# Softmax heads: 640 key columns per query tile in PSUM banks of 384 and 256 columns instead of 512 and 128

## The chip, the cores and the metric

The kernel runs on one core of one Trainium2 chip. The metric is the device time of one execution in microseconds; the lower the better. The times given are medians of runs on the same chip.

## The reference, cut to what matters

One encoder layer over 2048 positions of width 1024: an adaLN-modulated RMS norm, one input projection, two groups of eight attention heads of width 64, an output projection, and an MLP of width 4096. The first group is stick-breaking attention ("SB" in the kernel), the second is chunked softmax attention ("CA"). The change is in the second group:

```python
qc = q.reshape(B, nc, CHUNK, H, d)                      # CHUNK = 64
s = jnp.einsum('bnqhd,bnkhd->bnhqk', qc, k_band) * (d ** -0.5)   # own chunk + 8 before: 576 keys
s = s + bias[None, None]                                # learned, by clipped relative position
s = jnp.where(valid[None, :, None, None, :], s, NEG_INF)
p = jax.nn.softmax(s, axis=-1)
out = jnp.einsum('bnhqk,bnkhd->bnqhd', p, v_band)
```

Two chunks of 64 queries make a query tile of 128 rows. Their bands, one chunk apart, cover 640 keys together, and the bias table holds a large negative number where a row doesn't see a key. So a query tile of one head needs scores of 128 queries by 640 keys, a row minimum of the negated scores, an exponential, a row sum and a division.

## The kernel before, in words

The kernel is written with a tile framework that assigns buffers, semaphores and the order of most engines' instructions; TensorE instructions are kept in the order in which the program writes them (`pe = Ordered(tc, nc.tensor)`). SyncE's DMA issues in the attention part (`sp = nc.sync`) are not, so the scheduler may place them differently when anything around them changes.

The positions are held in reversed order in four blocks of 512 (`g` = 0 to 3). The attention part is a list of units. A unit is one head and one block `g` of queries (for SB also one block of keys), and it has four steps `qi`, one query tile of 128 rows each. Units come in this order: SB of blocks 2 and 3, CA of blocks 2 and 3, SB of block 1, CA of block 1, SB of block 0, CA of block 0. The CA units of blocks 0, 1 and 2 see 640 keys in each step: 8 heads times 3 blocks make 24 such units and 96 such steps. Those of block 3 have at most 512 keys per step, all in one bank; there are 8 of these units.

The main loop runs one step of a "front" unit, whose scores and softmax are computed, and one of a "back" unit, eight steps behind, whose probabilities are transposed on TensorE (`transposes`), split into two fp32r halves on ScalarE and VectorE (`parts`: tiles `wth`, `wtl`), and multiplied with the values (`values`, tile `acc`). One turn of the loop writes to TensorE, in this order: the transposes of the back unit (up to two tiles `wt` of four 128-column transposes), up to two pairs of value products, the scores of the next front step (`scores`), and a few matmuls of a dense "filler" job (the projections of later blocks, tiles `pf` and `po`), whose number is planned ahead and not decided at run time.

All score and transpose tiles (`z`, `cz`, `ct`, `wt`) come from one PSUM pool of four banks with the tag "z". A bank holds 512 fp32 columns. A new tile takes a bank that the program has released, and its first matmul waits until the last reader of that bank is done.

The scores of a 640-key step lie in two places. `scores(qi)` writes the first 512 keys into a tile `cz` of its own (two matmuls of 512 columns: the queries' high and low halves against the keys). The last 128 keys, the "tail", lie in a tile `ct`, and all four tails of a unit share one bank: `scores(0)` writes them with eight matmuls of 128 columns ahead of `cz`. VectorE reads them with a fused instruction that subtracts the scores from the bias and keeps the row minimum: `tail(qi)` for the tail (tile `s`, from `ct`), and in `soft1(qi)` one for `cz`, which takes the tail's minimum as its start. `soft1(0)` does `tail(0)`, `cz(0)`, `tail(1)`; `soft1(1)` does `cz(1)`, `tail(2)`, and so on; so the `ct` bank is held from `scores(0)` until `tail(3)`, which stands in `soft1(2)`. ScalarE then does the exponential over all 640 columns (tile `e`), GpSimd the division.

All of these instructions carry line L42 in the profile, the line of the helper that records the ordering; they are told apart by their tiles.

Of the kernel before, what the change touches and what calls it, by code (L numbers as in the profile page):

```python
# [9 lines left out]
F32 = mybir.dt.float32  # L10
# [8 lines left out]
P = 128  # L19
# [6 lines left out]
TB = 512  # L26
# [53 lines left out]
def encoder_kernel(ctx, tc, xT, c, g1, g2, w_in, w_rest, gqk, bias, w_o, w1, w2, w_ada, b_ada, out):  # L80
# [2 lines left out]
    pe = Ordered(tc, nc.tensor)  # L83
    osp = Ordered(tc, nc.sync)

    WIN = 640
    cpool = ctx.enter_context(tc.tile_pool(name="cpool", bufs=1))
    dram = ctx.enter_context(tc.tile_pool(name="dram", bufs=1, space=DRAM))
    rp = ctx.enter_context(tc.tile_pool(name="rp", bufs=2))
# [5 lines left out]
    pz = ctx.enter_context(tc.tile_pool(name="pz", bufs=4, space=PSUM))  # L95
# [5 lines left out]
    def scratch(name, shape, *counts):  # L101
        return {i: dram.tile(shape, F32, name=name + "_".join(map(str, i))) for i in product(*map(range, counts))}
# [8 lines left out]
    scr_wo = scratch("scr_wo", [P, 2, KT, P], KT)  # L111
    scr_b = scratch("scr_b", [P, WIN], NH)
    scr_h = dram.tile([P, KT, 2, TB], F32, name="scr_h")
# [19 lines left out]
    def column(tag):  # L133
        small[tag].append(small[tag].pop(0))
        return small[tag][-1]
# [103 lines left out]
    if True:  # L239
# [183 lines left out]
        def prepare_bias(h):  # L423
            b = stp.tile([P, WIN], F32, tag="bg", name=f"b{h}", bufs=2)
            sp.dma_start(b, bias[h])

            def rest():
                pool.memset(b[0:HD, WIN - HD :], NEG)
                pool.memset(b[HD:P, 0:HD], NEG)
                sp.dma_start(scr_b[h,], b)  # L430

            behind.add(4, rest)
# [245 lines left out]
    if True:  # L678
# [16 lines left out]
        def load_k(ca, h, tb, n, nm):  # L695
            k = (kp1 if ca else kp0).tile([P, n * TB], F32R, tag=f"k{ca}", name=f"k{ca}_{h}_{nm}")
            r = (h % 2) * HD
            for i in range(n):
                for l in range(2):
                    ldq.dma_start(  # L700
                        k[l * HD : (l + 1) * HD, i * TB : (i + 1) * TB].bitcast(F32),
                        scr_k[ca, tb + i, h // 2][l, r : r + HD],
                    )
            return k
# [42 lines left out]
        class Unit:  # L747


            def __init__(self, h, g, first, last):  # L750
                self.h, self.g, self.first, self.last = h, g, first, last
                self.nm = f"{self.ca}_{h}_{g}"
                self.ws = []
                self.wt = {}
# [30 lines left out]
        class SB(Unit):  # L785
# [27 lines left out]
            def scores(self, qi):  # L813
                nm = f"{self.nm}_{qi}"
                c0 = qi * P if self.diag else 0
                n = TB - c0
                self.z = z = pz.tile([P, TB], F32, tag="z", name=f"z{nm}")
                qs = slice(qi * P, (qi + 1) * P)
                pe.matmul(z[:, :n], self.q[:, 0, qs], self.k[:, c0:], start=True, stop=False)
                pe.matmul(z[:, :n], self.q[:, 1, qs], self.k[:, c0:], start=False, stop=True)  # L820
# [28 lines left out]
        class CA(Unit):  # L849
            ca = 1  # L850

            def __init__(self, h, g):
                super().__init__(h, g, True, True)
                self.weight = 0.9 * (1 if g < NTB - 1 else 0.75)
                self.nk = min(2 * TB, S - g * TB)
                order = [3] + [kb for kb in (4, 2, 1, 0, 5, 6, 7) if kb < self.nk // P]
                self.blocks = [(kb, max(0, kb - 4), min(4, kb + 1)) for kb in order]

            def load(self):
# [6 lines left out]
                self.k = load_k(1, h, g, nk // TB, f"{g}")  # L866
                self.bt = op.tile([P, WIN], F32, tag="bias", name=f"bias{h}_{g}", bufs=2)
                n = min(WIN, nk)
                sp.dma_start(self.bt[:, :n], scr_b[h,][:, :n])
# [7 lines left out]

            def size(self, qi):
                n = min(WIN, self.nk - qi * P)
                return n, min(n, TB)  # L880

            def scores(self, qi):
                nm = f"{self.nm}_{qi}"
                n, hn = self.size(qi)
                if qi == 0 and n > hn:
                    self.tails = pz.tile([P, TB], F32, tag="z", name=f"ct{nm}")
                    for i in range(STEPS):
                        t = self.tails[:, i * P : (i + 1) * P]
                        ks = slice(i * P + TB, i * P + WIN)
                        for l in range(2):  # L890
                            pe.matmul(t, self.q[:, l, i * P : (i + 1) * P], self.k[:, ks], start=l == 0, stop=l == 1)
                self.z = z = pz.tile([P, TB], F32, tag="z", name=f"cz{nm}")
                ks = slice(qi * P, qi * P + hn)
                for l in range(2):
                    pe.matmul(z[:, :hn], self.q[:, l, qi * P : (qi + 1) * P], self.k[:, ks], start=l == 0, stop=l == 1)

            def tail(self, qi):
                nm = f"{self.nm}_{qi}"
                n, hn = self.size(qi)
                s = zp.tile([P, WIN], F32, tag="p", name=f"s{nm}")  # L900
                m = 3e38
                if n > hn:
                    m = column("m0")
                    t = self.tails[:, qi * P : (qi + 1) * P]
                    dve.tensor_tensor_reduce(s[:, hn:n], t, self.bt[:, hn:n], -1.0, 3e38, ALU.add, ALU.min, m)
                self.sm[qi] = (s, m)

# [240 lines left out]
        STEPS = 4  # L1148
# [145 lines left out]
    if True:  # L1294
# [349 lines left out]
        def plain(mb, i):  # L1644

            f = len(steps)
            steps.extend(Second(mb, i, j) for j in range(NP))
            spread = lambda *ns: [f + n for n in ns]
            if i == 6:
                update(mb, 0, 1, spread(0, 1, 2, 8), spread(4, 5, 6, 12))  # L1650
            if i == 5:
                update(mb, 1, 1, spread(1, 2, 3, 9), spread(6, 7, 8, 13))
                wide = []

                def slot(nm):
                    if not wide:
                        t = raw_pair([P, HK, TB], F32, nm)
                        wide.extend(t[:, n, :] for n in range(HK))
                    return wide.pop(0)

                if mb:
                    update(mb, 0, 0, spread(11, 11, 11, 11), spread(16, 16, 17, 17), slot)
                    update(mb, 1, 0, spread(13, 13, 14, 14), spread(18, 18, 19, 19), kept)
                else:
                    update(mb, 0, 0, spread(11, 12, 13, 14), spread(16, 17, 18, 19))
                    update(mb, 1, 0, spread(15, 16, 17, 21), spread(20, 21, 22, 25), None, True)
            return f
# [115 lines left out]
        def outer(i, plan):  # L1783

            f = len(steps)
            steps.extend(Outer(i, q, k) for q in range(7) for k in range(HP))
            for g in range(HP // 2):
                for pr, (begin, gap) in plan["load"].items():
                    at(begin + gap * g, lambda pr=pr, g=g: half(i, pr, g))
                for pr, (begin, gap) in plan["sum"].items():  # L1790
                    at(begin + gap * g, lambda pr=pr, g=g: half_sum(i, pr, g))
            for q in range(7):
                at(f + HP * q - 12, steps[f + HP * q].load)
            for pr, b in ((5, "22"), (6, "12"), (2, "11"), (4, "21")):
                s = steps[f + HP * OUTER.index(pr)]
                at(f + HP * OUTER.index(pr) + 1, lambda s=s, b=b: s.load_x(b))
            return f
# [47 lines left out]
        for mb in (1, 0):  # L1845
# [3 lines left out]
            for j in range(NP):  # L1849
                f = steps[begin + 7 * j]  # L1850
# [33 lines left out]
        f = plain(0, 1)  # L1884
# [4 lines left out]
        for i, p in ((7, 6), (2, 5), (3, None), (4, None)):  # L1889
            f = outer(i, plan)  # L1890
# [109 lines left out]
```

## Time and profile before

| | before |
|---|---|
| median of 3 runs | 2568.27 us (2566.47 to 2568.61) |
| the profiled execution's own time | 2568.92 us |
| its span, first to last instruction | 2567.2 us |
| TensorE busy | 2534.1 us, 99% |
| VectorE busy | 2012.0 us, 78% |
| ScalarE busy | 1496.2 us, 58% |
| GpSimd busy | 760.8 us, 30% |
| `ct` matmuls, 128 columns | 192 |
| `cz` matmuls, 512 columns | 208 |

Busy time of an engine is the union of its instructions' spans. A TensorE matmul's span is longer than the distance to the next one's start, since they overlap; the cost of a matmul in a stream is the distance between starts, which can be had from a run of n matmuls as (union minus one span) / (n - 1). Of the 208 `cz` matmuls of 512 columns, 192 belong to the 24 units with tails, 16 to block 3.

### The profile page before, as it was taken

The numbers are of one execution on the slowest core, as the hardware profiler recorded it, in microseconds if no ns is written. First come the engines' busy times: TensorE is split into PE (matmuls) and PEld (weight loads), VectorE is DVE, ScalarE is ACT, GpSimd is POOL, SyncE is SP. The second block draws the span as 40 slices with busy tenths as digits, with TensorE's granted clock in tenths as the row PEclk, the third lists the DMA queues.
The fourth block names the chain that finished last, engine by engine and source line by source line (L and its number), as shares of the span: only waits on it lengthen the run. The fifth ranks groups of instructions, "written<-read, shape, count | busy, mean of one in ns | idle before, by whom it ended". The sixth has DMA issues, their size and how long they took to land.

```text
span 2567.2 us, 39419 instructions
## 1 busy us (share of the span) xinstructions
PE 2534.1 (99%) x12436; PEld 2109.1 (82%) x12436; DVE 2012.0 (78%) x3501; ACT 1496.2 (58%) x2871; POOL 760.8 (30%) x1136
## 2 busy tenths in 40 slices
PE   9999999999999999999999999999999999999999
PEld 7888888888888888887887888888888878788887
DVE  7656767887789878998867777668978657988897
ACT  6333435668866687666755555566555545646565
POOL 4330145776776667777612000000000000000000
PEclk9999999999999999999999999999999999999999
DMA  9879978689877788756786888787899779677872
GB/s 351 332 298 363 342 281 293 213 237 290 277 239 233 238 279 272 248 193 196 224 309 243 286 285 274 260 306 267 275 323 304 273 254 409 246 272 265 291 268 82
DMA packets 293200, 698.92 MB, mean 272 GB/s; under 512 B 31360, under 2 KB 83584, under 8 KB 281856
## 3 DMA queue, kind: packets, MB, share of 16 engines
q1 hardware_dynamic: 291696, 691.69, 78.1%
q10 hardware_dynamic: 1296, 4.72, 0.5%
q8 instruction: 98, 1.61, 0.2%
q14 instruction: 110, 0.90, 0.1%
HBM read 477.66 MB, written 218.63 MB: 271 GB/s over the span
## 4 chain that ended last, share of the span: by engine, by line
PE 86%; DVE 5%; ACT 3%; DMA 2%; issue 2%; POOL 1%; SPq 1%; DVEq 0%; POOLq 0%; ACTq 0%
PE ps L42 29%; PE ps_s L42 14%; PE pt L42 11%; PE acc L42 6%; PE wt L42 6%; PE po L42 4%; PE z L42 4%; PE pf L42 4%; PE pq L42 3%; PE cz L42 2%; DVE p L42 2%; PE pso L42 1%; DVE opr L42 1%; PE ct L42 1%; ACT z L42 1%
## 5 line engine op out<-in xcount | busy, mean ns | idle before, releaser
L42 PE MATMUL ps<-h,opw 128*128 128x512 f32 x1512 | 361.7, 392 | 3.6 <-ACT cp L42 3.6
L42 ACT CAST wth<-wt 128x512 fp32r<-128x512 f32 (+3 forms) x544 | 257.4, 484 | 172.4 <-PE wt L42 162.5
L42 POOL TENSOR_TENSOR b<-p 128x512 f32<-128x512 f32 (+1 forms) x320 | 292.5, 914 | 167.9 <-DVE p L42 91.9
L42 PEld LDWEIGHTS ps<-h,opw 128*128 128x128 f32 x1512 | 285.7, 189 | 63.6 <-ACT cp L42 4.0
L42 DVE TENSOR_TENSOR wtl<-wt,wth 128x512 fp32r<-128x512 f32 (+3 forms) x544 | 291.2, 547 | 59.2 <-ACT wth L42 56.7
L42 PE MATMUL pt<-w,ht 128*128 128x512 f32 x1248 | 288.2, 391 | 0.0
L42 PE MATMUL ps_s<-h,opw 128*128 128x512 f32 x1152 | 278.6, 391 | 3.2 <-ACT ps_s L42 3.2
L42 PEld LDWEIGHTS pt<-w,ht 128*128 128x128 f32 x1248 | 233.0, 188 | 47.7
L42 PE MATMUL ps<-oph,opv 128*128 128x512 f32 x1152 | 263.8, 391 | 2.5 <-DVE txo L42 2.5
L42 DVE TENSOR_TENSOR_SCAN p<-z,p,zero 128x512 f32<-128x512 f32 x192 | 245.7, 1281 | 25.6 <-ACT z L42 18.6
L42 PEld LDWEIGHTS ps_s<-h,opw 128*128 128x128 f32 x1152 | 217.1, 189 | 48.8 <-ACT ps_s L42 3.6
L42 PEld LDWEIGHTS ps<-oph,opv 128*128 128x128 f32 x1152 | 217.2, 189 | 48.4 <-DVE txo L42 3.0
L42 PE MATMUL acc<-wth,v 128*128 128x512 f32 (+3 forms) x544 | 220.5, 409 | 0.0
L42 ACT CAST opr<-r 128x512 fp32r<-128x512 f32 x224 | 139.3, 623 | 107.7 <-PE ps L42 51.1
L42 ACT ACTIVATE z<-z 128x512 f32<-128x512 f32 (+1 forms) x320 | 166.5, 521 | 55.2 <-PE z L42 49.3
L42 PE MATMUL z<-k,q 128*128 128x512 f32 (+3 forms) x640 | 185.6, 372 | 7.7 <-DVE p L42 7.2
L42 PE MATMUL acc<-wtl,v 128*128 128x512 f32 (+3 forms) x544 | 185.4, 347 | 0.0
L42 PE MATMUL ps<-opr,ol 128*128 128x512 f32 x768 | 176.4, 389 | 0.1
L42 DVE TENSOR_TENSOR opr<-r,opr 128x512 fp32r<-128x512 f32 x224 | 151.2, 688 | 27.5 <-ACT opr L42 24.8
L42 PE MATMUL wt<-ident,b 128*128 128x128 f32 x1088 | 171.4, 273 | 1.1 <-DVE cols L42 0.3
L42 PEld LDWEIGHTS wt<-ident,b 128*128 128x128 f32 x1088 | 136.3, 140 | 42.2 <-DVE cols L42 1.8
L42 PEld LDWEIGHTS ps<-opr,ol 128*128 128x128 f32 x768 | 144.0, 188 | 30.5 <-DVE ol L42 0.4
(218 smaller groups left out, 4862.8 us busy)
## 6 DMA issues: line engine op xcount, KB each, us to landing
q<-scr_q SPq DMA_DIRECT2D x128, 256.0 KB, 4.7
w<-in_w_dram SPq DMA_DIRECT2D x64, 512.0 KB, 5.8
r<-scr_hid SPq DMA_DIRECT2D x64, 512.0 KB, 7.5
k<-scr_k SPq DMA_DIRECT2D x240, 128.0 KB, 4.3
v<-scr_v SPq DMA_DIRECT2D x120, 256.0 KB, 3.9
wa<-in_w_ada_dram SPq DMA_DIRECT2D x48, 512.0 KB, 6.4
ow<-scr_wo SPq DMA_DIRECT2D x24, 1024.0 KB, 5.8
hw<-scr_hid SPq DMA_DIRECT2D x48, 512.0 KB, 6.4
```

The source lines that it names most:

```text
L42: return lambda *x, **y: self.tc.keep_in_program_order(f(*x, **y))
```

## The change

A step of more than 512 keys is cut at 384 columns (`NEAR`) instead of at 512. The `cz` tile gets the first 384 keys, and the tail is the other 256. Two tails fill a bank, so a unit has two `ct` tiles: `scores(0)` writes the tails of steps 0 and 1, and `scores(1)` those of steps 2 and 3, in each case ahead of that step's own `cz`. The number of matmuls per unit stays at eight for the tails and eight for `cz`, and so does the number of columns that they stream (8 x 640). The VectorE instructions stay the same in number and order, with 256 and 384 columns in place of 128 and 512. A step of at most 512 keys is left as it was: one bank.

```diff
-    WIN = 640
+    WIN, NEAR = 640, 384
...
+                self.tails = {}
...
                 n = min(WIN, self.nk - qi * P)
-                return n, min(n, TB)
+                return n, NEAR if n > TB else n

             def scores(self, qi):
                 nm = f"{self.nm}_{qi}"
                 n, hn = self.size(qi)
-                if qi == 0 and n > hn:
-                    self.tails = pz.tile([P, TB], F32, tag="z", name=f"ct{nm}")
-                    for i in range(STEPS):
-                        t = self.tails[:, i * P : (i + 1) * P]
-                        ks = slice(i * P + TB, i * P + WIN)
+                if qi < 2 and n > hn:
+                    ct = pz.tile([P, 2, WIN - NEAR], F32, tag="z", name=f"ct{nm}")
+                    for i in (2 * qi, 2 * qi + 1):
+                        self.tails[i] = t = ct[:, i % 2, :]
+                        ks = slice(i * P + NEAR, i * P + WIN)
                         for l in range(2):
                             pe.matmul(t, self.q[:, l, i * P : (i + 1) * P], self.k[:, ks], start=l == 0, stop=l == 1)
                 self.z = z = pz.tile([P, TB], F32, tag="z", name=f"cz{nm}")
...
                 if n > hn:
                     m = column("m0")
-                    t = self.tails[:, qi * P : (qi + 1) * P]
+                    t = self.tails.pop(qi)
                     dve.tensor_tensor_reduce(s[:, hn:n], t, self.bt[:, hn:n], -1.0, 3e38, ALU.add, ALU.min, m)
```

The built program's order on TensorE differs in nothing but the second `ct` group of each of the 24 units; VectorE, ScalarE and GpSimd keep their order. On SyncE the scheduler places some loads and stores of the attention part a few positions earlier or later.

## The prediction

> **What bounds the kernel now.** I read the page's busy times and slices first, then the three stretches in which the changed units run, then the groups by shape inside them, then TensorE's waits, and last the timeline of single units.
>
> ```profile
> PE 2534.1 (99%) x12436; PEld 2109.1 (82%) x12436; DVE 2012.0 (78%) x3501; ACT 1496.2 (58%) x2871; POOL 760.8 (30%) x1136
> ...
> PE   9999999999999999999999999999999999999999
> ...
> PE 86%; DVE 5%; ACT 3%; DMA 2%; issue 2%; POOL 1%; SPq 1%; DVEq 0%; POOLq 0%; ACTq 0%
> ```
>
> TensorE is busy in every slice and carries 86% of the chain that ended last. A shorter stream on TensorE is then worth its own length, wherever nothing else runs late in the same stretch. The softmax units with tails lie in three stretches (eight units in each; those of block 3, which stay as they are, lie among the first eight):
>
> ```profile
> core 0: us, PE busy (x) PEld busy (x) DVE busy (x) ACT busy (x) POOL busy (x), PEclk, DMA share, GB/s
> 571.00:701.00 130.00, 126.76 (x773) 108.55 (x772) 95.73 (x357) 107.43 (x268) 92.76 (x92) 1.00 0.92 287
> 883.00:961.00 78.00, 77.39 (x470) 66.19 (x470) 60.61 (x219) 61.00 (x139) 50.76 (x41) 1.00 0.90 279
> 1208.00:1291.00 83.00, 82.89 (x516) 72.19 (x515) 64.83 (x226) 62.53 (x144) 54.75 (x48) 1.00 0.67 204
> ```
>
> The granted clock is 1.00 throughout. TensorE idles 3.24 us in the first, 0.61 in the second and 0.11 in the third. The next engine, ScalarE in the first two and VectorE in the third, is at 83%, 78% and 78%. So the second and third stretch are TensorE's alone; in the first something else is sometimes late. What it is, the waits of that stretch and one place in its timeline say:
>
> ```profile
> PE cz L42 <- DVE cols L42: 1.7, 3, 1.0
> PE wt L42 <- DVE cols L42: 1.4, 2, 1.1
> ...
> 597.68 0.59 ACT L42 CAST stf<-pf 128x512 fp32r<-128x512 f32 x1
> 598.30 0.69 DVE L42 TENSOR_TENSOR stf<-pf,stf 128x512 fp32r<-128x512 f32 x1 [2.58 <-ACT stf L42]
> 598.91 0.74 DVE L42 CUSTOM_DVE_ANT_0 s<-cz,bias,cols 128x512 f32<-128x512 f32 x1
> 599.80 0.41 PE L42 MATMUL wt<-ident,e 128*128 128x128 f32 x2 [1.05 <-DVE cols L42]
> ```
>
> Five waits, 3.1 us, all for a bank that VectorE's score instruction had not yet read. In the one shown VectorE had stood 2.58 us behind ScalarE's eviction of a filler tile, and everything behind it in VectorE's order came late.
>
> **The matmuls.** These are the groups that the change touches, with the two shapes that take their place; block 3 runs those already, with the same operands:
>
> ```profile
> L42 PE MATMUL cz<-k,q 128*128 128x512 f32 x208 | 67.2, 404 | 0.4 <-DVE cols L42 0.4
> L42 PE MATMUL ct<-k,q 128*128 128x128 f32 x192 | 24.8, 272 | 0.7 <-DVE p L42 0.7
> L42 PE MATMUL cz<-k,q 128*128 128x384 f32 x16 | 4.1, 338 | 0.0
> L42 PE MATMUL cz<-k,q 128*128 128x256 f32 x16 | 3.3, 288 | 0.4 <-DVE cols L42 0.4
> ...
> L42 PEld LDWEIGHTS ct<-k,q 128*128 128x128 f32 x192 | 24.2, 191 | 2.5 <-DVE p L42 1.2 <-DVE cols L42 0.3
> ```
>
> The second figure before the bar is one matmul's span, which overlaps the next one's; the distance between starts is the cost. `cz` comes in pairs, `ct` in runs of eight:
> - 512 columns: 67.2 / 104 = 0.646 us for a pair, less 0.404 = 0.242 us.
> - 384 columns: 4.1 / 8 = 0.5125, less 0.338 = 0.1745 us.
> - 256 columns: 3.3 / 8 = 0.4125, less 0.288 = 0.1245 us.
> - 128 columns: 24.8 / 24 = 1.033 for eight, less 0.272, over 7 = 0.109 us.
>
> From 512 to 256 columns the distance falls almost with the columns; from 256 to 128 it falls only from 0.1245 to 0.109. The weight loads of `ct` say why: 24.2 / 24 = 1.008 for eight, less 0.191, over 7 = 0.117 us from load to load. Each of these matmuls has weights of its own, and a 128-column one is over before the next weights are in.
>
> Per unit, eight `cz` matmuls gain 8 x (0.242 - 0.1745) = 0.54 us and eight `ct` matmuls lose 8 x (0.1245 - 0.109) = 0.12 us: 0.41 us gained. Times 24 units: 9.9 us.
>
> The Trainium skill speaks against this: "TensorE: Matmul & The Clock Gate", section "Back-to-back issue gap", gives the isolated distance as N/2.4 + 2.5 ns, in proportion to the columns N, and both kernels stream 5120 columns per unit; by that rule alone the gain would be nothing. The trace does not agree at the short end: 0.109 us at 128 columns, where the rule would have 0.056. The same page's section "LDWEIGHTS (loading the stationary operand)" gives P/1.2 ns, 107 ns for 128 columns of weights, and with that floor the trace agrees.
>
> **VectorE.** The same number of instructions in the same order, with other widths:
>
> ```profile
> L42 DVE CUSTOM_DVE_ANT_0 s<-cz,bias,cols 128x512 f32<-128x512 f32 x96 | 71.7, 747 | 4.5 <-PE cz L42 2.4 <-PE wt L42 0.2
> L42 DVE CUSTOM_DVE_ANT_0 s<-ct,bias 128x128 f32<-128x128 f32 x96 | 27.5, 286 | 4.0 <-PE ct L42 3.2 <-POOL p L42 0.7
> L42 DVE CUSTOM_DVE_ANT_0 s<-cz,bias 128x512 f32<-128x512 f32 x8 | 5.5, 681 | 0.0
> L42 DVE CUSTOM_DVE_ANT_0 s<-cz,bias 128x384 f32<-128x384 f32 x8 | 4.4, 548 | 0.0
> L42 DVE CUSTOM_DVE_ANT_0 s<-cz,bias 128x256 f32<-128x256 f32 x8 | 3.3, 415 | 0.0
> ```
>
> A start value from a column costs 747 - 681 = 66 ns. Before: 286 + 747 = 1033 ns per step. After: 415 for the tail and 548 + 66 = 614 for `cz`: 1029. Nothing in the sum. Inside a unit 130 ns move: the tail of the next step, which stands behind `cz` in a step, gets longer, and `cz`, whose end frees its bank and lets the exponential start, gets shorter. ScalarE's and GpSimd's instructions are untouched.
>
> **The banks.** Before, `cz` of step 1 waits until VectorE has read `cz` of step 0. After, the second `ct` takes that bank, and `cz` of step 1 takes the first `ct`'s, which is free only after `tail(1)`, the next instruction on VectorE. That is the one added wait, 24 times. Behind it on TensorE, in order, stand that step's fillers and the next step's transposes; VectorE and ScalarE wait for these. A usual unit, the first of a stretch and one that waits already show the cover:
>
> ```profile
> 587.59 1.00 PE L42 MATMUL ct<-k,q 128*128 128x128 f32 x8
> 588.63 0.29 DVE L42 CUSTOM_DVE_ANT_0 s<-ct,bias 128x128 f32<-128x128 f32 x1 [0.67 <-PE ct L42]
> 589.15 0.75 DVE L42 CUSTOM_DVE_ANT_0 s<-cz,bias,cols 128x512 f32<-128x512 f32 x1 [0.22 <-PE cz L42]
> 589.82 0.29 DVE L42 CUSTOM_DVE_ANT_0 s<-ct,bias 128x128 f32<-128x128 f32 x1
> 590.87 0.62 PE L42 MATMUL cz<-k,q 128*128 128x512 f32 x2
> ...
> 883.89 0.75 DVE L42 CUSTOM_DVE_ANT_0 s<-cz,bias,cols 128x512 f32<-128x512 f32 x1 [0.24 <-PE wt L42]
> 884.37 0.63 PE L42 MATMUL cz<-k,q 128*128 128x512 f32 x2
> ...
> 903.25 0.75 DVE L42 CUSTOM_DVE_ANT_0 s<-cz,bias,cols 128x512 f32<-128x512 f32 x1
> 903.92 0.29 DVE L42 CUSTOM_DVE_ANT_0 s<-ct,bias 128x128 f32<-128x128 f32 x1
> 904.06 0.73 PE L42 MATMUL cz<-k,q 128*128 128x512 f32 x2 [0.23 <-DVE cols L42]
> ```
>
> In the unit at 588, `scores(0)` shrinks from 8 x 0.109 + 2 x 0.242 = 1.36 us to 4 x 0.1245 + 2 x 0.1745 = 0.85, so TensorE reaches the second `ct` at 590.87 - 0.51 = 590.36, and `cz` of step 1 one `ct` group later, at 590.86. VectorE, which waited 0.67 us for all eight tails, gets the first four matmuls 0.37 us earlier; even with no gain there `tail(1)` ends by 590.11 + 0.13 = 590.24. The wait is covered by 0.6 us. In the unit at 904 TensorE already waits for VectorE. There the second `ct` starts at about 904.0, takes 0.50 us, and `tail(1)`, now 415 ns long, ends at 904.34 inside that time: the added wait costs nothing, but the time saved ahead of it only lengthens the old one, and that unit gains nothing.
>
> That is the loss I set against the gross gain: six waits of this kind (the five and this one). If each eats a unit's 0.41 us, 2.5 us; if VectorE moves with TensorE, none. I take half, 1.2. In the first unit of each stretch, where `cz` of step 1 had a bank that was long free, it now waits for `cz` of step 0: at 884, VectorE is done with that at 884.64, and TensorE gets there at 884.37 - 0.51 + 0.50 = 884.36. That is 0.28 us each if VectorE is no earlier, nothing if it is (less than nothing is excluded, since no wait goes there); I take 0.4 for the three.
>
> **DMA.** SyncE's loads and stores in the attention part move by a few positions. A store that waits for its data holds up the loads behind it, but TensorE loses next to nothing to loads now:
>
> ```profile
> PE po L42 <- DMA ow<-scr_wo: 1.0, 1, 1.0
> ```
>
> It is TensorE's one wait for a load in the attention part. I take nothing, with 1 us to either side for the range.
>
> **Sum.** 9.9 - 1.2 - 0.4 = 8.3 us. From the profiled execution's 2568.9 that gives 2560.6; that execution lies 0.65 us above the median of the three runs, 2568.27, so the forecast for the median is 2560.0 us.
>
> **The rivals.**
> - Swallowed. The first stretch, with ScalarE at 83%, gives nothing back: its waits re-anchor TensorE on VectorE about every 20 us, and each unit's saving turns into a longer wait; the second stretch gives half. For it speaks that the waits are there; against it, that long runs of the first stretch have none and that VectorE and ScalarE wait for TensorE as well (0.67 and 0.22 in the rows above), so they come earlier with it. Gain 3.3 + 1.7 = 5.0, less the 0.4: 4.6, and 2563.7; with the second stretch gone too, 2565.4.
> - The columns decide. If 128 columns cost what their share of 512 does (0.242 / 4 = 0.06 us), eight `ct` and eight `cz` matmuls cost the same before and after: 2568.3. The rows of `ct` matmuls and weight loads, 0.109 and 0.117, speak against it.
> - Slower: the added wait decides. If VectorE, late as at 598, brings `tail(1)` in each unit more than 0.41 us after TensorE could have started `cz` of step 1, the gain is gone; at the 1.05 us of the wait shown, 24 x (1.05 - 0.41) = 15 us, 2584. Against it speak 0.6 us of cover in the usual unit, the unchanged sum on VectorE, and that the second `ct` group runs just ahead of the wait.
>
> **How the numbers follow.** What a measurement of this kernel can tell from no change is about 0.2%, 5.1 us; the bounds are 2563.1 and 2573.4. Forecast with its own scatter 0.78; swallowed 0.12; columns 0.04; slower 0.06. The range takes in the full 9.9 us with 1 us for the loads, 2557.4, and the swallowed case with the second stretch gone, 2565.4. Faster by over 0.2%: 0.79 (the forecast and a little of the swallowed); same 0.15; slower 0.06.
>
> **What would show it.** Right: `cz` of 384 columns with 0.175 us and `ct` of 256 with 0.125 us from start to start, TensorE's busy time 8 to 10 us lower, each of the three stretches shorter by 2 to 3.3 us, VectorE's sum unchanged. Wrong: TensorE's waits for `cols` grown in the first stretch by what the matmuls save (swallowed); `ct` of 256 columns at over 0.17 us (columns); a wait of `cz` for `cols` in nearly every unit (slower).

## The result and the profile after

| | before | after |
|---|---|---|
| median, 19 runs each | 2568.32 us (2565.39 to 2573.41) | 2561.97 us (2558.99 to 2566.52) |
| ratio | | 0.9974, 95% interval 0.9968 to 0.9981 |
| span of the profiled execution | 2567.2 us | 2560.3 us |

The change is 6.4 us faster by the medians, 0.26% by the ratio. The forecast was 8.3 us. A second measurement, on another chip (below), gave 3.3 us: both intervals exclude no change, but the size of the gain, a quarter of a per cent or less, is not far above what single runs scatter by.

The page after, busy time by engine (before, TensorE 2534.1 and VectorE 2012.0):

```profile
PE 2526.9 (99%) x12436; PEld 2109.4 (82%) x12436; DVE 2009.3 (78%) x3501; ACT 1496.6 (58%) x2871; POOL 760.3 (30%) x1136
```

The same count of instructions, 7.2 us less of TensorE. The groups by shape that take the place of the 512 and 128 columns (union of spans, mean span of one, idle time before them), TensorE and then VectorE:

```profile
L42 PE MATMUL cz<-k,q 128*128 128x384 f32 x208 | 54.7, 344 | 0.4 <-DVE cols L42 0.3
L42 PE MATMUL ct<-k,q 128*128 128x256 f32 x192 | 32.0, 290 | 1.7 <-DVE cols L42 1.0 <-DVE p L42 0.7
...
L42 DVE CUSTOM_DVE_ANT_0 s<-cz,bias,cols 128x384 f32<-128x384 f32 x96 | 58.6, 610 | 4.0 <-PE wt L42 0.5 <-PE cz L42 0.2
L42 DVE CUSTOM_DVE_ANT_0 s<-ct,bias 128x256 f32<-128x256 f32 x96 | 40.2, 418 | 1.8 <-PE ct L42 1.5 <-issue 0.3
```

`cz` costs 54.7 / 104 - 0.344 = 0.182 us from start to start (0.1745 forecast). `ct` runs in fours now: 32.0 / 48 = 0.667, less 0.290, over 3 = 0.126 (0.1245 forecast). VectorE has 610 + 418 = 1028 ns per step (1029 forecast).

Where the time went is best read between the same two TensorE instructions of both kernels, which stand in the same order. In the third stretch, from the first unit's first tail product to the last unit's, before and after:

```profile
1205.36 1.11 PE L42 MATMUL ct<-k,q 128*128 128x128 f32 x8 [0.73 <-DVE p L42]
1274.99 1.06 PE L42 MATMUL ct<-k,q 128*128 128x128 f32 x8
```

```profile
1201.31 0.74 PE L42 MATMUL ct<-k,q 128*128 128x256 f32 x4 [0.73 <-DVE p L42]
1268.88 0.69 PE L42 MATMUL ct<-k,q 128*128 128x256 f32 x4
```

69.63 us became 67.57: 2.1 us for seven units. The table does this for each whole stretch, from the TensorE instruction at 568, 880 and 1204 us of the trace of before to the one at 701, 961 and 1292 us, and for the same two instructions in each kernel run below; every distance between two starts is put down to the group of the earlier instruction.

| us | stretch 1 | stretch 2 | stretch 3 | sum | against before |
|---|---|---|---|---|---|
| before | 132.86 | 80.79 | 87.80 | 301.45 | |
| the change | 131.24 | 79.15 | 85.82 | 296.21 | -5.24 |
| the change, second profile | 131.23 | 79.17 | 85.81 | 296.21 | -5.24 |
| 448 and 192 columns | 132.06 | 79.81 | 86.86 | 298.73 | -2.72 |
| 512 and 128, banks of the change | 133.77 | 80.71 | 88.57 | 303.05 | +1.60 |
| own columns first in step 1 | 129.57 | 78.79 | 85.93 | 294.29 | -7.16 |
| the same, second profile | 130.74 | 78.81 | 85.89 | 295.44 | -6.01 |
| half of the tail products left out | 128.50 | 76.96 | 83.91 | 289.37 | -12.08 |
| tails as products of 128 | 136.05 | 83.68 | 91.25 | 310.98 | +9.53 |
| own columns first, copy on VectorE | 136.76 | 81.22 | 89.60 | 307.58 | +6.13 |
| before, VectorE relieved | 130.38 | 80.13 | 87.72 | 298.23 | -3.22 |
| the change, VectorE relieved | 127.85 | 76.81 | 85.59 | 290.25 | -11.20 |

In the change `cz` lost 3.5, 4.1 and 3.6 us in the three stretches and `ct` gained 1.3, 1.4 and 1.1: 7.3 us less in the two groups, of which 5.2 came out at the ends of the stretches (72%). The two profiles of the change agree in each stretch within 0.02 us. The rest of the difference between the two spans lies where nothing was changed: 0.9 us at the start, before the first changed unit, and 0.8 us after the attention part. That part moves from run to run; in the second profile of the change it went 1.8 us the other way.

### The profile page after: what moved, and what is told of

It is laid out like the page before. It is cut to its first block, busy times and chain, and to the rows that moved or that the text cites. A ratio compares the mean times of both kernels' runs of the same rounds, so it can differ in the third digit from the quotient of the medians.

```text
span 2560.3 us, 39412 instructions
## 1 busy us (share of the span) xinstructions
PE 2526.9 (99%) x12436; PEld 2109.4 (82%) x12436; DVE 2009.3 (78%) x3501; ACT 1496.6 (58%) x2871; POOL 760.3 (30%) x1136
## 4 chain that ended last, share of the span: by engine, by line
PE 81%; DVE 8%; DMA 4%; ACT 3%; issue 3%; POOL 1%; SPq 1%; DVEq 0%; ACTq 0%; POOLq 0%
PE ps L42 25%; PE ps_s L42 12%; PE pt L42 11%; PE acc L42 6%; PE wt L42 6%; PE pf L42 4%; PE po L42 4%; PE z L42 4%; PE pq L42 3%; DMA scr_hid<-to 2%; DVE p L42 2%; PE pso L42 1%; PE cz L42 1%; PE ct L42 1%; DMA w<-in_w_dram 1%
```

## The experiments

My theory: a product's cost can't fall below what the load of its weights takes, and under about 256 columns it is set by that load and no longer by its columns; call this the floor. The change takes the tails off the floor, and waits for VectorE swallow part of the gain. The rivals: the widths don't matter, and the gain (or a loss) comes from where banks and loads came to lie; or the added wait is the price that counts.

**Another width.** `NEAR` 448.

```diff
-    WIN, NEAR = 640, 384
+    WIN, NEAR = 640, 448
```

> Cut at 448 and 192 columns, two tails to a bank as in the change. If the gain is the floor that the weight loads set under narrow matmuls: 448 columns cost halfway between the 0.247 us of 512 before and the 0.187 of 384 after, 0.217, and 192 columns lie near the floor, 0.12 (between 0.109 and 0.129); per unit 8 x (0.217 + 0.12) = 2.70 us against 2.85 before and 2.53 after, so a bit under half of the gain: 2565 to 2566.5 us, ratio to before 0.9985 to 0.9993. If the gain came from the new places of the banks or of the loads and not from the widths, the full gain, 2562. If columns cost alike at any width and the banks do nothing: 2568.

2564.11 us, ratio 0.9981 (0.9972 to 0.9990) to 2569.65 before on that chip. That is 1 us below the time expected, and the interval takes in the change's 0.9974 as well: as a time it doesn't tell half of the gain from all of it. The stretches do: they show just over half, 2.72 of 5.24 us. By shape:

```profile
L42 PE MATMUL cz<-k,q 128*128 128x448 f32 x192 | 56.6, 376 | 0.6 <-DVE cols L42 0.5
L42 PE MATMUL ct<-k,q 128*128 128x192 f32 x192 | 29.5, 276 | 1.6 <-DVE cols L42 0.8 <-DVE p L42 0.7
```

192 columns cost (29.5 / 48 - 0.276) / 3 = 0.113 us, no more than 128 columns with 0.109. The floor reaches beyond 192 columns; it ends between there and 256 (0.126 in the change).

**The banks alone.** `NEAR` 512: the old widths in the new arrangement.

> The widths of before (512 and 128) with the change's two tail tiles, the second written in step 1, the added wait and its loads' order. If the widths make the gain: no gain, and the price of 24 more group heads and waits shows, 0 to 1.5 us: 2568 to 2570 us, ratio 1.0000 to 1.0006. If the bank places or the loads' order make it: 2562.

2569.89 us, ratio 1.0001 (0.9993 to 1.0010). The rival of the banks and loads falls: the arrangement alone gains nothing. In the stretches it costs 1.6 us. Where, the timeline of one of its units shows (`cz` rows hold two products; the second figure is their union):

```profile
1216.14 0.56 PE L42 MATMUL ct<-k,q 128*128 128x128 f32 x4
1216.53 0.68 PE L42 MATMUL cz<-k,q 128*128 128x512 f32 x2
1218.41 0.56 PE L42 MATMUL ct<-k,q 128*128 128x128 f32 x4
1218.81 0.67 PE L42 MATMUL cz<-k,q 128*128 128x512 f32 x2
1220.91 0.62 PE L42 MATMUL cz<-k,q 128*128 128x512 f32 x2
```

A pair right behind a run of 128-column products takes 0.67 or 0.68, another one 0.62. The old kernel paid this once per unit, the new arrangement with narrow tails pays it twice: 24 x 0.05 = 1.2 us. Behind tails of 256 columns it is gone, as the change's trace shows in the same way:

```profile
905.48 0.51 PE L42 MATMUL cz<-k,q 128*128 128x384 f32 x2
906.57 0.69 PE L42 MATMUL ct<-k,q 128*128 128x256 f32 x4
907.10 0.51 PE L42 MATMUL cz<-k,q 128*128 128x384 f32 x2
```

So part of the floor's price stood in the old kernel's `cz` group, next to the tails and not in them.

**The floor by itself.** Each tail product of the change as two of 128 columns.

```diff
-                        for l in range(2):
-                            pe.matmul(t, ..., self.k[:, ks], start=l == 0, stop=l == 1)
+                        for c in range(2):
+                            kc = slice(ks.start + c * P, ks.start + (c + 1) * P)
+                            for l in range(2):
+                                pe.matmul(t[:, c * P : (c + 1) * P], ..., self.k[:, kc], start=l == 0, stop=l == 1)
```

> The change with each 256-column tail product written as two of 128 columns: the same columns, the same banks, 384 small matmuls in place of 192. If weight loads set a floor near 0.112 us: 192 x (0.224 - 0.129) = 18 us more of TensorE's stream, of which a few us only take the place of waits: 2575 to 2580 us. If columns alone count: 2562.

2578.81 us, ratio 1.0046 (1.0032 to 1.0060), against 2565.07 for the change on the same chip: 13.7 us more, 14.8 in the stretches. The columns and the banks are the same; what is added is 192 products on the floor. It also settles the rival of the prediction by which columns alone decide.

```profile
L42 PE MATMUL ct<-k,q 128*128 128x128 f32 x384 | 49.1, 271 | 1.1 <-DVE p L42 0.7 <-DVE cols L42 0.3
```

(49.1 / 48 - 0.271) / 7 = 0.107 us for each.

That it is the load of the weights, and neither the columns nor a fixed time per product, a group that both kernels have anyway shows: products of one single column, each with 128 x 128 weights of its own. In the trace of before:

```profile
1211.84 0.95 PE L42 MATMUL pvm<-ones,r 128*128 128x1 f32 x8
1211.62 1.08 PEld L42 LDWEIGHTS pvm<-ones,r 128*128 128x128 f32 x8
```

Eight of them take 0.95 us; eight of 128 columns took 1.00 in the unit at 588. Their loads follow one another at 0.112 us, and so do the products, with one column as with 128, but for the first pair: the first product started late, behind the filler product ahead of it, the second one's load had begun by then, and the second product followed after 0.026 us. So a product can follow another that fast; the 0.112 us go from load to load.

**The added wait.** In step 1 the unit's own `cz` ahead of the second tails, so that it takes the bank that it took before the change.

```diff
-                if qi < 2 and n > hn:
+                if qi == 0 and n > hn:
                     (tails of steps 0 and 1)
                 self.z = z = pz.tile([P, TB], F32, tag="z", name=f"cz{nm}")
...
+                if qi == 1 and n > hn:
+                    (tails of steps 2 and 3)
```

> The change with step 1's own 384 columns written ahead of the second pair of tails, so that they take the bank they took before the change, and the tails take the first tail tile's. If the added wait costs little, as I hold: the same as the change within 1 us, 2561 to 2563, ratio to before 0.997 to 0.998. If the added wait eats a good part of the gain: 2559.5 or less.

2561.10 us, ratio 0.9967 (0.9954 to 0.9979). Run again beside the change itself:

> The change as it is, on the same chip as the next kernels: 6 to 7 us under the kernel before, ratio 0.9972 to 0.9977. Nothing here tells the theories apart; it is the base for the others.

> Step 1's own columns ahead of the second tails, now beside the change on one chip. If the second tails' place and wait cost what the traces of the three stretches show (294.3 us in all against 296.2 in the change): 1 to 2 us under the change. If that difference was chance between two profiles: within 0.5 us of the change.

The change 2565.07 us, 0.9987 (0.9977 to 0.9996), half of the 6 to 7 us expected; own columns first 2562.87 us, 0.9981 (0.9972 to 0.9990). The intervals overlap, so as times the two can't be told apart. In the stretches this order was 1.9 and 0.8 us shorter, most of it in the first; it was 0.1 longer in the third. It is the best of the full kernels tried, by an amount that isn't shown.

**How much of a saving comes out.**

> The change without the products of the queries' low halves with the 256 tail keys: this leaves 96 of the 192 tail matmuls out, 96 x 0.129 = 12.4 us of TensorE's stream in the same three stretches. It measures how much of a saving there reaches the end. If three quarters do, as in the change (5.3 us off the three stretches for 7.3 us less in the two groups): 9 us below the change, 2553. If all of it does: 2549.6. If the stretches are near the limit of VectorE and ScalarE, so that more saving turns into waits: 2557 or more.

2554.43 us, ratio 0.9945 (0.9933 to 0.9958). The `ct` group of the stretches fell from 24.8 to 14.0 us, 10.8 less; the stretches fell by 6.8. So 63% came out, less than the 72% of the change (5.24 of 7.3). TensorE's idle time in the three stretches together was 4.85 us before, 5.88 in the change and 7.65 here: the further TensorE gets ahead, the more turns into waits.

**Which engine swallows it.** First the wrong guess, ScalarE. One of the two copies that end a softmax unit goes to VectorE:

```diff
-            act.copy(o[rows, :], u.acc[rows, :])
+            (dve.tensor_copy if u.ca else act.copy)(o[rows, :], u.acc[rows, :])
```

> The kernel with step 1's own columns first, and one of the two copies that end a softmax unit moved from ScalarE to VectorE (64 partitions, 512 columns, 0.58 us each, 32 of them). If ScalarE being late in the first stretch swallows part of the saving: its waits shrink and 0.5 to 2 us more come out, about 2559 to 2560. If VectorE is the late one, the copy only adds to it: 1 to 4 us slower than without the move.

2574.43 us, ratio 1.0027 (1.0016 to 1.0037): 11.6 us slower than without the move. The copies and the waits that they brought:

```profile
L42 DVE COPY o<-acc 64x512 f32<-64x512 f32 x32 | 22.0, 688 | 22.6 <-ACT otmp L42 21.7 <-POOL os L42 0.6
...
DVE o L42 <- ACT otmp L42: 21.7, 24, 1.4
PE cz L42 <- DVE cols L42: 9.4, 15, 1.2
```

VectorE copies for 22 us and stands another 22 us behind ScalarE's first copy, with its score instructions queued behind; TensorE's waits of `cz` for them grow from 2.7 (without the move) to 9.4 us. I had expected 1 to 4 us of loss, for the copies alone; the waits were not in it. So the run shows that what delays VectorE reaches TensorE here. It doesn't show what ScalarE's lateness by itself costs, since the move brought a wait for ScalarE with it. Then the reverse, VectorE relieved in both kernels:

```diff
+                if self.ca:
+                    act.copy(wh[:, cols], wt[:, cols])
+                    self.wt[j] = (wh, wh, cols, kb)
+                    return
```

> The kernel before, with VectorE relieved: in the softmax units the low half of the transposed probabilities is left out, and the value product that used it takes the high half a second time, so TensorE's stream is the same and VectorE has 240 subtractions less, 0.3 to 0.7 us each. TensorE's waits for VectorE in the three stretches go: they take 297 to 299 us in all instead of 301.5. If these waits are not VectorE's: 301.

> The change with the same relief. If VectorE, late in places, swallows the rest of the saving: the three stretches take 7 to 8 us less than in the kernel before with the same relief, about the 7.3 us that the two groups' own distances fell by, against 5.2 without the relief. If the rest is lost elsewhere (ScalarE, GpSimd, the order of the matmuls): again about 5.

(There are 224 such subtractions, not 240. Leaving them out also takes VectorE out of what the value products and the transposes' banks wait for; the two effects aren't separated.) Before with relief: 2566.05 us, 0.9987 (0.9977 to 0.9997). The change with relief: 2557.47 us, 0.9953 (0.9936 to 0.9970). That is 8.6 us between the two on one chip. The stretches fall by 298.23 - 290.25 = 8.0 us instead of 5.2, and the groups `cz` and `ct` by 8.3 instead of 7.3: nearly all of it comes out. TensorE's waits for the score instructions, in the change and in the change with relief:

```profile
PE cz L42 <- DVE cols L42: 1.9, 4, 1.1
PE wt L42 <- DVE cols L42: 1.0, 1, 1.0
PE ct L42 <- DVE cols L42: 1.0, 2, 0.8
```

```profile
PE wt L42 <- DVE cols L42: 0.4, 1, 0.4
```

So it was VectorE that swallowed 2.7 us, in the first two stretches (1.6 and 1.6 us gained without relief, 2.5 and 3.3 with it). In the third it hardly matters: 2.0 and 2.1. There the groups fell by 2.5 us, and nearly all of the half microsecond that is missing lies in one place. The last filler product ahead of the transposes of one step is 0.67 us from the next start, where it is 0.23 elsewhere. In the change the transposes wait for VectorE's `wtl`; with relief, at the same place, their weight load waits for GpSimd's division `e`:

```profile
1269.76 0.40 PE L42 MATMUL po<-fx,ow 128*128 128x512 f32 x1
1270.43 1.06 PE L42 MATMUL wt<-ident,e 128*128 128x128 f32 x8 [0.27 <-DVE wtl L42]
```

```profile
1264.60 0.86 PEld L42 LDWEIGHTS wt<-ident,e 128*128 128x128 f32 x8 [0.45 <-POOL e L42]
```

Take one late engine away there, and the next stands right behind it.

## Why the prediction was right, and where its sizes were off

*The floor.* Right, and shown: 0.107 us by itself, the same distance with one column, half of the gain at half of the way, none from the arrangement.

*The gross gain, 9.9 us.* Right for the usual product, too high for the sum: the two groups fell by 7.3. From start to start the median `cz` product of the 24 units takes 0.234 us before and 0.176 in the change, the median `ct` product of 256 columns 0.120. (The 0.242 that I took for 512 columns was too high for the usual one: 32 of those 104 pairs stand behind products of 128 columns, with 0.285 from the first to the second.) Worked out with these medians, and with 0.05 us for each pair behind the tails, the groups should fall by 192 x (0.234 - 0.176) + 24 x 0.05 - 192 x (0.120 - 0.109) = 10.2 us. Most of the rest is in few, long distances. In the change 11 of the 192 `cz` products and 20 of the 192 `ct` products take over 0.02 us longer than the median, 3.7 us too much together; before, the pairs behind the tails left out, 10 do, with 1.5 us. Part of them stand at a wait; of others the view of waits shows nothing. Ten are the first `ct` product right behind value products of 128 columns: 0.17 us instead of 0.12, with VectorE relieved as well. The prediction has no term for these.

*The loss to waits, 1.2 us.* Right mechanism, and the term that was mis-sized most: 2.1 us outside of the two groups, besides what the long distances took inside them. About half of the 2.1 shows as idle time of TensorE (4.85 to 5.88 us). The place named for it is one where it shows. In the unit that stood at 904 us before, the second `ct` now waits 0.75 us for the first `cz`'s bank, and the added wait behind it costs nothing, as worked out (`tail(1)` ends at 901.21, four `ct` products start at 900.93, and `cz` starts at 901.51):

```profile
900.25 0.62 DVE L42 CUSTOM_DVE_ANT_0 s<-cz,bias,cols 128x384 f32<-128x384 f32 x1
900.79 0.42 DVE L42 CUSTOM_DVE_ANT_0 s<-ct,bias 128x256 f32<-128x256 f32 x1
900.93 0.74 PE L42 MATMUL ct<-k,q 128*128 128x256 f32 x4 [0.75 <-DVE cols L42]
901.51 0.51 PE L42 MATMUL cz<-k,q 128*128 128x384 f32 x2
```

I took half of six waits; waits also came where there had been none.

*The added wait, 0.4 us.* Neither shown nor refuted: with the order swapped, the stretches are 0.8 to 1.9 us shorter, but the two can't be told apart as times. In the usual unit, at 588 before and at 586 in the change, the cover was there: VectorE's second tail instruction ended at 588.20, and `cz` of step 1 started at 589.21.

```profile
587.78 0.42 DVE L42 CUSTOM_DVE_ANT_0 s<-ct,bias 128x256 f32<-128x256 f32 x1
...
588.73 0.64 PE L42 MATMUL ct<-k,q 128*128 128x256 f32 x4
589.21 0.52 PE L42 MATMUL cz<-k,q 128*128 128x384 f32 x2
```

*VectorE unchanged, DMA at nothing.* Both held: 1028 ns per step, and TensorE's wait for a load went from 1.0 to 0.2 us.

*The rivals.* "Swallowed" is real, as a part: VectorE takes 2.7 of 8.0 us, though the first stretch still gave 1.6 us, where that rival gave it nothing. What ScalarE takes by itself is open. "The columns decide" is refuted by the tails cut into products of 128; "slower" needs a wait of `cz` for `cols` in nearly every unit, and the trace of the change has four in all.

*The signs.* Two of those that were to show it right came out low: TensorE's busy time fell by 7.2 us, not 8 to 10, and the stretches got shorter by 1.6, 1.6 and 2.0 us, not by 2 to 3.3. So the forecast has the mechanism; that the first measurement came as near to its 8.3 us as 6.4 is partly luck: 1.7 us of the difference between the two profiled spans lie outside of the changed units, and the second measurement, 3.3 us, would have counted as no change by the 0.2% that I had set.

## What to carry to other kernels

Where products of 128 rows of weights each follow one another, count their number as well as their columns: here a product below some 200 columns cost the same as one of 128, so an uneven cut of a width should leave no piece under that floor. A saving on an engine that is busy 99% of the time comes out only as far as the next engine keeps up at that place: here 5.2 of 7.3 us, and 8.0 of 8.3 with that engine relieved. And a price per instruction should be taken apart into the usual one, from the median, and the few long ones, from those that stand in the same company, behind the same neighbours and under the same waits.

## What the runs showed of the hardware that was not expected

A product of one column, with weights of its own, takes as long as one of 128: 0.112 us from start to start in both. The floor leaves a trace behind it: a 512-column product right after a run of 128-column ones needs about 0.05 us more (pairs of 0.67 to 0.68 us against 0.62), which is not seen after 256-column ones (0.51 and 0.51). And 192 columns cost no more than 128 to within 0.004 us (0.113 and 0.109).
